# An encoder layer's gate projection cut into four blocks of 960 columns instead of three of 1024 and three chunks

## The chip, the cores and the metric

The kernel runs on one core of a Trainium2 chip. The metric is the device time of one execution in microseconds; the median of three runs of the kernel before is 1906.27 us (1906.04 to 1908.03). The engines are called as in the profile: PE is the matrix engine (PEld its weight loads), DVE the vector engine, ACT the scalar engine, POOL and SP the two others; SP issues nearly all DMAs here.

## What is computed

One encoder layer on 256 tokens of width 4096, all in float32: an input projection, two groups of attention heads, an output projection `w_out`, then a gated per-layer embedding and a last normalisation. The change is in the gated embedding and what follows it:

```python
    x = x + jnp.einsum('bse,ed->bsd', jnp.concatenate([y_a, y_b], axis=-1), w_out[i])

    ple = jnp.einsum('bsc,cd->bsd', p[i], w_ple[i])
    gate = jax.nn.sigmoid(jnp.einsum('bsd,de->bse', rms_norm(x, g_ple[i]), w_ple_gate[i]))
    x = x + ple * gate
return rms_norm(x, g_final)
```

`w_ple_gate` is 4096 x 4096 and `w_ple` 256 x 4096. The gate is (256 x 4096) times (4096 x 4096), the last large product of the kernel.

## The kernel before

**Products in three passes.** Every float32 operand is split into a high half (`hi`, a rounded copy made by ACT) and a low half (`lo`, the difference, made by DVE). A product is the sum of three matmuls: hi x hi, lo x hi, hi x lo (function `mm`). A product here takes 128 rows of contraction (one `kt`, 32 of them), one of the two halves t=0, 1 of the tokens (128 each), and up to 512 columns of weights.

**Steps.** The work is a list of steps. A step loads a piece of weights by DMA into one of four `raw` buffers (`RAW = 4`), converts it to hi and lo into a pair of a ring (three `wp` pairs and, in the gate's blocks, two more slots, `Al2` and `B0`), and multiplies it. A plain step of a block of 1024 columns takes one `kt`: 128 rows by 1024 columns, four products (two token halves, two column halves; PSUM banks M2, X, M3, M4), 12 matmuls.

**Seven products for eight.** In a `Block`, a pair of `kt` can be computed with seven products instead of eight (Winograd's form of Strassen's scheme): four short steps M1, M2 M3, M5 M7, M6 M4, marked `f` in the order. DVE forms four differences of the weights for it, and the sums of the left operand (`x1_sums`, slots `Al0`, `B5`, `Ah1`, `Ah0`) are shared by all blocks. When the last fast product is done, `wide_mid` copies M1 out of its bank and makes four additions; at the end of the block `wide_done` adds the four plain sums, applies tanh (for the sigmoid), multiplies by the embedding and adds to x1, one quarter (128 tokens x 512 columns) at a time, with the sum of squares by ACT in `ss2`. `spread(n, lead, trail, extra)` makes the order of a block: `lead` plain steps, n pairs interleaved with plain steps, `trail` plain steps, and the w_ple step `e` inserted.

**The gate before.** Three blocks of 1024 columns with 7 pairs each, lead 6, trail 4; then a chunk of 512 columns (c=6), a chunk of 256 (c=7) and a chunk of 256 (c=8), all plain (class `Chunk`, whose steps are `Old`). The last chunk runs token half t=0 over all 32 `kt`, keeps the converted weights (`kept`), and then runs t=1, so that t=0's final normalisation (`finish`) and its writes go beside the products of t=1. x1 lies in eight tiles `T0` to `T7` of 512 columns each.

**The end.** `late_gain(c)` multiplies x1's tile c by g_final, loaded by SP (`load_g`) into the slots `Al0` and `B5` once the sums there are dead; behind the last product, `finish(t)` computes the reciprocal root of the mean square by small DVE operations and scales the eight tiles by it (five and the last halves on DVE, two on ACT), each followed by a DMA to the output.

**What sets the order.** Each engine runs its instructions in the order in which they are written out. At build time a small clock in the kernel (`Clock`, with assumed durations) decides when a conversion or a side task is written: `lead` says how many steps ahead conversions may go, `tick` and `advance` let side tasks in, and late gains only when there is slack. So a wait in one engine's list holds up everything behind it there. All operations are recorded by one helper line, L176, and are told apart by tile names without numbers: `hi`, `lo` and `raw` are the ring and load buffers, `m`, `s`, `o`, `t` PSUM banks, `T` the tiles of x1, `B`, `Ah`, `Al`, `Q`, `junk` slots of the SBUF, `st` small statistics.

Of the kernel before, what the change touches and what calls it, by code (L numbers as in the profile page):

```python
# [18 lines left out]
P = 128  # L19
S = 256  # L20
# [177 lines left out]
class Chunk:  # L198
# [4 lines left out]
    def __init__(self, src, nk, n, lhs, banks, done, needs=lambda j: (), per=2, ts=(0, 1), keep=None):  # L203
        self.src, self.nk, self.n, self.lhs, self.banks = src, nk, n, lhs, banks
        self.done, self.needs, self.per, self.ts, self.keep = done, needs, per, ts, keep
        self.ps, self.ring, self.ring_id, self.row = None, WP, None, lambda j: j
# [3 lines left out]
def encoder_layer(ctx: ExitStack, tc: tile.TileContext, x, p, positions, g_mix, w_in, g_q_latent, w_uq,  # L210
# [823 lines left out]
    ss1, ss2 = (stat(NT * n).rearrange("p (t c) -> p t c", t=NT) for n in (8, 9))  # L1034
# [73 lines left out]
    class Step:  # L1108
# [6 lines left out]
        def __init__(self, load, split, run, needs=(), frees=0, time=2.73):  # L1115
            self.load, self.split, self.run, self.needs, self.frees, self.after = load, split, run, needs, frees, None
            self.hold, self.mid = 0, False
            self.time = time
# [4 lines left out]
    class Block:  # L1123
# [9 lines left out]
        def __init__(self, w, lhs, sums, name, order, needs, tags, tmp, ring):  # L1133
# [8 lines left out]
        def step(self, which, *args):  # L1142
            new = Step(*args)
            new.holds = self.holds if which == "M1" else ()
# [11 lines left out]
        def load(self, kt):  # L1156
            kt = self.row(kt)
            r = clock.made(wp.tile([P, 2, Q], F32, tag="raw", name=f"raw_{kt}", bufs=RAW), "raw", RAW)
            for lo, n in ((0, Q), (Q, Q)) if self.late and kt == 16 else ((0, 2 * Q),):
# [24 lines left out]
        def fast_steps(self, j):  # L1184
# [9 lines left out]
            def split1(hi, lo):  # L1194
                if isinstance(self.tmp, tuple):
                    T.extend(slot(b, [2, Q]) for b in self.tmp)
                else:
                    both = slot(self.tmp, [4, Q])
# [122 lines left out]
    blocks = [(512 * c, 512) for c in range(7)] + [(3584, 256), (3840, 256)]  # L1321
    FAST, WIDE = 7, 3
# [21 lines left out]
    def load_g(c):  # L1344
        if not gF:
            gF.extend(slot(tag, [2048]) for tag in ("Al0", "B5"))
# [4 lines left out]
    WIDE_PLE = [dict(zip(((0, 0), (0, 1), (1, 0), (1, 1)), (*PAIRS[2 - k], "t0", "t1"))) for k in range(3)]  # L1351

    def wide_ple(k):
# [3 lines left out]
        def step(kt):  # L1357
            box = []

            def load():  # L1360
                box.append(clock.made(wp.tile([P, 2, Q], F32, tag="raw", name=f"raw_e{kt}", bufs=RAW), "raw", RAW))
                nc.sync.dma_start(box[0].rearrange("p a b -> p (a b)"),
                                  w_ple[kt * P:(kt + 1) * P, 1024 * k:1024 * (k + 1)])

            def run(hi, lo):
                for (t, h), tag in WIDE_PLE[k].items():
                    if kt == 0:
                        ps[t, h] = bank(tag, [Q])
# [5 lines left out]
            return Step(load, lambda hi, lo: split(hi, lo, box[0]), run, ["pT", ("mid", k)], 1)  # L1374

        def out():
            for h in range(2):
                nc.scalar.activation(P4[0, h], ps[0, h], AF.Copy)
# [4 lines left out]

    def wide_mid(k, blk):

        def task():
            e = blk.e = slot("B1", [4, Q])
# [8 lines left out]
    def wide_done(k, blk):  # L1396
        def task():
            e, ps = blk.e, blk.ps
            quarters = ((0, 0, 0, "M2"), (3, 1, 1, "X"), (1, 0, 1, "M3"), (2, 1, 0, "M4"))
            for i, t, h, m in quarters:  # L1400
                nc.vector.tensor_tensor(e[:, i], e[:, i], ps[m], op=ALU.add)
# [594 lines left out]
```

## Time and profile before

| | us |
|---|---|
| median of three runs | 1906.27 |
| profiled execution | 1906.09 |
| its span on the core | 1904.3 |
| PE busy | 1886.7 |
| DVE busy | 1667.5 |
| ACT busy | 1125.3 |
| last product to the end of the span | 12.3 |

The span is from the first to the last instruction; the execution takes 1.8 us more around it. The granted TensorE clock is 0.998 of full speed. A row of the timeline has the start in us, the length, the engine, line, operation, output <- inputs, the shape and a count of merged instructions; a bracket tells how long the engine was idle before it and what released it. Rows of PE show a modelled length that overlaps the next matmul, so the distance between starts is what a matmul costs. A row of a group has the count, the busy time in us, the mean in ns, and the idle time before.

### The profile page before, as it was taken

What the parts mean: (1) busy time and instruction counts of PE and PEld (TensorE: products, weight loads), DVE (VectorE), ACT (ScalarE), POOL (GpSimd) and SP (SyncE); (2) the same over time, 40 slices, a digit from 0 to 9 for tenths busy, and PEclk for the clock granted to TensorE, in tenths of its full rate; (3) what the DMA queues carried; (4) which work ended last, traced back from release to release, by engine and by line L of the source; (5) the groups of instructions that cost most, each with busy time, mean ns of one, the idle gap of its engine ahead of it and who ended that gap; (6) DMA issues with size and microseconds to landing.
All of it is one profiled execution on the core that took longest, in us unless ns stands there. A gap on an engine that the chain in (4) does not pass through costs nothing.

```text
span 1904.3 us, 25920 instructions
## 1 busy us (share of the span) xinstructions
PE 1886.7 (99%) x9430; PEld 1598.9 (84%) x9430; DVE 1667.5 (88%) x2320; ACT 1125.3 (59%) x1523; POOL 29.5 (2%) x41
## 2 busy tenths in 40 slices
PE   9999999999999999999999999999999999999997
PEld 7888888888898888888888999888888888888887
DVE  6999999898878899999998777799988989989865
ACT  7655556564567766556555555656655556665643
POOL 0000000000000000000000011000000000000000
PEclk9999999999999999999999999999999999999999
DMA  8666666666645466676667543566666666666575
GB/s 278 188 207 212 214 215 200 194 217 189 190 139 147 146 196 196 196 216 188 210 199 210 135 131 119 175 216 214 218 203 214 186 201 221 195 216 192 190 234 177
DMA packets 156904, 370.61 MB, mean 195 GB/s; under 512 B 28860, under 2 KB 62760, under 8 KB 156776
## 3 DMA queue, kind: packets, MB, share of 16 engines
q1 hardware_dynamic: 156216, 367.11, 61.9%
q0 software_dynamic: 512, 1.84, 0.3%
q8 instruction: 74, 1.21, 0.3%
q14 instruction: 54, 0.44, 0.1%
q10 hardware_dynamic: 48, 0.02, 0.0%
HBM read 364.72 MB, written 4.19 MB: 194 GB/s over the span
## 4 chain that ended last, share of the span: by engine, by line
PE 89%; DVE 7%; issue 1%; ACT 1%; DMA 1%; DVEq 0%; ACTq 0%
PE m L176 53%; PE t L176 16%; PE s L176 11%; PE o L176 9%; DVE B L176 2%; DVE T L176 2%; DVE lo L176 2%; DMA raw<-in_w_in_dram 1%; ACT hi L176 0%; DVE st L176 0%; ACT T L176 0%; ACT B L176 0%; DVE Al L176 0%; DVE Ah L176 0%; ACT Ah L176 0%
## 5 line engine op out<-in xcount | busy, mean ns | idle before, releaser
L176 ACT ACTIVATE hi<-raw 128x1024 fp32r<-128x1024 f32 (+2 forms) x429 | 412.8, 971 | 303.2 <-PE m L176 96.7
L176 DVE TENSOR_TENSOR lo<-raw,hi 128x1024 fp32r<-128x1024 f32 (+2 forms) x429 | 473.3, 1113 | 87.9 <-ACT hi L176 85.9
L176 PE MATMUL m<-hi,Ah 128*128 128x512 f32 (+2 forms) x764 | 279.9, 379 | 0.1
L176 PE MATMUL m<-hi,Al 128*128 128x512 f32 (+2 forms) x756 | 268.9, 370 | 0.0
L176 PE MATMUL m<-lo,Ah 128*128 128x512 f32 (+2 forms) x643 | 238.6, 371 | 0.7 <-DVE lo L176 0.5
L176 DVE TENSOR_TENSOR B<-raw,B 128x1024 fp32r<-128x1024 f32 (+2 forms) x215 | 199.8, 942 | 17.4 <-ACT B L176 15.8
L176 PE MATMUL m<-hi,B 128*128 128x512 f32 (+1 forms) x678 | 209.2, 364 | 0.0
L176 ACT ACTIVATE B<-raw 128x1024 fp32r<-128x1024 f32 (+1 forms) x131 | 125.2, 965 | 92.9 <-DMA raw<-in_w_in_dram 29.3
L176 PEld LDWEIGHTS m<-hi,Ah 128*128 128x128 f32 x764 | 143.9, 188 | 23.3 <-ACT hi L176 0.6
L176 PEld LDWEIGHTS m<-hi,Al 128*128 128x128 f32 x756 | 141.9, 188 | 23.7
L176 PEld LDWEIGHTS m<-hi,B 128*128 128x128 f32 x678 | 124.3, 189 | 19.7
L176 PEld LDWEIGHTS m<-lo,Ah 128*128 128x128 f32 x643 | 121.2, 189 | 20.4 <-DVE lo L176 2.4
L176 PE MATMUL m<-lo,B 128*128 128x512 f32 (+1 forms) x339 | 123.1, 363 | 0.0
L176 PE MATMUL m<-B,Ah 128*128 128x512 f32 (+1 forms) x427 | 112.7, 363 | 0.4 <-DVE B7b L176 0.4
L176 DVE TENSOR_TENSOR T<-raw,T 128x512 f32<-128x512 f32 (+2 forms) x107 | 85.2, 808 | 5.5 <-ACT T L176 3.9
L176 PE MATMUL m<-B,Al 128*128 128x512 f32 (+1 forms) x323 | 88.8, 351 | 0.0
L176 PEld LDWEIGHTS m<-B,Ah 128*128 128x128 f32 x427 | 73.4, 189 | 13.0 <-DVE B7b L176 0.8
L176 PE MATMUL t<-hi,Ah 128*128 128x512 f32 (+1 forms) x201 | 75.5, 388 | 0.0
L176 ACT ACTIVATE hi<-B 128x1024 fp32r<-128x1024 f32 x53 | 55.5, 1058 | 28.1 <-PE m L176 8.4
L176 PEld LDWEIGHTS m<-lo,B 128*128 128x128 f32 x339 | 64.0, 189 | 9.6 <-DVE lo L176 0.2
L176 DVE TENSOR_TENSOR lo<-B,hi 128x1024 fp32r<-128x1024 f32 x53 | 63.5, 1219 | 2.9 <-ACT hi L176 2.7
L176 PE MATMUL t<-lo,Ah 128*128 128x512 f32 (+1 forms) x167 | 64.6, 387 | 0.0
(502 smaller groups left out, 4135.1 us busy)
## 6 DMA issues: line engine op xcount, KB each, us to landing
raw<-in_w_in_dram SPq DMA_DIRECT2D x359, 512.0 KB, 4.2
raw<-in_w_out_dram SPq DMA_DIRECT2D x128, 512.0 KB, 4.6
raw<-in_w_ple_gate_dram SPq DMA_DIRECT2D x128, 512.0 KB, 4.6
raw_q<-in_w_uq_dram SPq DMA_DIRECT2D x32, 256.0 KB, 3.6
raw_k<-in_w_ukv_dram SPq DMA_DIRECT2D x16, 512.0 KB, 4.1
T<-in_x_dram SPq DMA_DIRECT2D x13, 512.0 KB, 6.2
raw<-in_w_in_dram SPq DMA_DIRECT2D x16, 320.0 KB, 3.0
raw_r<-in_w_uq_dram SPq DMA_DIRECT2D x16, 256.0 KB, 3.6
```

The source lines that it names most:

```text
L176: return do(out, *rest, **named)
```

## The change

The gate becomes four blocks of 960 columns (two halves of 480, `HALF`) with 7, 7, 7 and 6 pairs, and one last chunk of 256 columns. The chunk of 512 and the first chunk of 256 go. Block k covers columns 960k to 960k+959; as x1's tiles are 512 wide, a quarter of 480 columns lies in one or two tiles (`x_parts`), and the sums of squares get 15 partial columns and the last chunk's. The fourth block has lead 5, trail 8, its w_ple step four steps before its end, its quarters in slot `Ah1` (from k=3), and gives up `Al2` and `B0` after its last fast step. The w_ple product of the last chunk goes between the seventh and eighth step of t=0, its halves in the slot of the first sums. The weights kept for t=1 go to other slots, the last of them into `raw` buffers. The g_final loads move into the fourth block, behind the fast step that frees each slot; `late_gain` is made for t=1 alone, five of eight inside the fourth block and three behind it, and `finish(0)` multiplies by r and g in one operation for each tile, all on DVE. In the trailing eight steps and behind them conversions may go nine steps ahead.

```diff
@@ class Block
-        def __init__(self, w, lhs, sums, name, order, needs, tags, tmp, ring):
+        def __init__(self, w, lhs, sums, name, order, needs, tags, tmp, ring, q=512):
+            self.q = q
...
-                self.ps[m] = bank(self.tags[m], [Q])
+                self.ps[m] = bank(self.tags[m], [self.q])
...
-            r = clock.made(wp.tile([P, 2, Q], F32, tag="raw", name=f"raw_{kt}", bufs=RAW), "raw", RAW)
+            r = clock.made(wp.tile([P, 2, self.q], F32, tag="raw", name=f"raw_{kt}", bufs=RAW), "raw", RAW)
...
@@ the gate's sizes
-    blocks = [(512 * c, 512) for c in range(7)] + [(3584, 256), (3840, 256)]
-    FAST, WIDE = 7, 3
+    FAST, WIDE, HALF = 7, 4, 480
+    E_AT = -4
+    FAST_P, LEAD_P, TRAIL_P = (7, 7, 7, 6), (6, 6, 6, 5), (4, 4, 4, 8)
+    END = 2 * WIDE * HALF
...
+    def x_parts(lo, n, t):
+        at, end, got = lo, lo + n, []
+        while at < end:
+            c = at // 512
+            to = min(end, 512 * (c + 1))
+            got.append((at // HALF + c, at - lo, x1[c][:, t, at - 512 * c:to - 512 * c]))
+            at = to
+        return got
...
-            e = blk.e = slot("B1", [4, Q])
+            e = blk.e = slot("Ah1" if k == WIDE - 1 else "B1", [4, HALF])
...
-                    nc.vector.tensor_tensor(xc, u, xc, op=ALU.add)
+                    for _, o, xc in x_parts((2 * k + h) * HALF, HALF, t):
+                        nc.vector.tensor_tensor(xc, u[:, o:o + xc.shape[1]], xc, op=ALU.add)
...
@@ the end
     def late_gain(c):
-        for t in range(NT):
-            nc.vector.tensor_tensor(x1[c][:, t], x1[c][:, t], g_cols(512 * c, 512), op=ALU.mult)
-            yield
-            yield
+        n = 512 if c < 7 else S
+        nc.vector.tensor_tensor(x1[c][:, 1, :n], x1[c][:, 1, :n], g_cols(512 * c, n), op=ALU.mult)
+        yield
...
         for c in range(8):
             xc = x1[c][:, t]
-            if c == 7:
+            if t == 0:
+                nc.vector.scalar_tensor_tensor(xc, xc, r, g_cols(512 * c, 512), op0=ALU.mult, op1=ALU.mult)
+            elif c == 7:
...
@@ the order
     for k in range(WIDE):
-        order = spread(FAST, 6, 4, (-1,))
-        blk = Block(w_ple_gate[:, 1024 * k:1024 * (k + 1)], lhs_x1, x1_s, "x1_sums", order,
-                    lambda kt: [("x1T", kt // 4)], LAST[k], "Ah2", WP + ["Al2", "B0"])
+        order = spread(FAST_P[k], LEAD_P[k], TRAIL_P[k], (-1 if k < WIDE - 1 else E_AT,))
+        blk = Block(w_ple_gate[:, 2 * HALF * k:2 * HALF * (k + 1)], lhs_x1, x1_s, "x1_sums", order,
+                    lambda kt: [("x1T", kt // 4)], LAST[k], "Ah2", WP + ["Al2", "B0"], HALF)
+        top = len(steps) + max(i for i, o in enumerate(order) if o == "f") if k == WIDE - 1 else 10 ** 6
         for tag in ("Al2", "B0"):
-            allow(blk, tag, lambda i: ran[0] >= out_end - 1)
+            allow(blk, tag, lambda i, top=top: ran[0] >= out_end - 1 and i < top)
...
+    for c in range(8):
+        at = fast[8 * (c // 4) + 11] + 1 + (2, 1)[c // 4] * (c % 4)
+        hook(at, lambda c=c: load_g(c))
+        hook(wide_end + 9 if c > 4 else at + 5, lambda c=c: spawn(late_gain(c), True))
+
+    def last(t):
+        return Chunk(cols(w_ple_gate, END, S), 32, S, lhs_x1, ("m2", "m3"), done_g(t), lambda j: (), per=4, ts=(t,),
+                     keep=(stay, t == 0))
+
+    ends = last(0)
+    add(ends, 0, 7)
...
+    add(small)
+    add(ends, 7)
+    add(last(1))
...
-        lead = i + AHEAD + (3 if len(step.ring) > 3 else max(0, min(3, i - (len(steps) - 25))))
+        lead = i + AHEAD + (7 if i > wide_end - TRAIL_P[-1] else 3 if len(step.ring) > 3 else 0)
```

More of the change, by code (lines that the diff above doesn't have):

```diff
@@ L1481, in done_g @@
+            nc.vector.scalar_tensor_tensor(u, u, 1.0, ple[t], op0=ALU.add, op1=ALU.mult)
+            nc.vector.tensor_tensor(xc, u, xc, op=ALU.add)
+            nc.vector.scalar_tensor_tensor(u, xc, 1.0, xc, op0=ALU.mult, op1=ALU.mult, accum_out=ss2[:, t, 15:16])
+            while "part2" not in flags:
+                yield
+            yield from finish(t)
         return task
     def late_gain(c):
[L1484 to L1487 removed]
+        n = 512 if c < 7 else S
@@ new lines, in last @@
+    def last(t):
[3 more added lines that the diff above has]
+    add(ends, 0, 7)
+    small = Chunk(cols(w_ple, END, S), 2, S, lambda kt: (pT[0][:, 0, kt], pT[0][:, 1, kt]), ("m0", "m1"), done_p,
+                  lambda j: ["pT", ("added", WIDE - 1)])
+    small.place = lambda: tuple(zs[0][:, i].rearrange("p (k a) c -> p k (a c)", k=2) for i in range(2))
+    add(small)
```

136 lines of the change are left out of this document (48 added, 88 removed).

## The prediction

> **What bounds the kernel now.** I read the busy shares first, then the shares of the chain of waits, then the busy time of each engine in six stretches (gate blocks 1, 2 and 3; the chunk of 512 and a little of the next; the two chunks of 256; the end).
>
> ```profile
> PE 1886.7 (99%) x9430; PEld 1598.9 (84%) x9430; DVE 1667.5 (88%) x2320; ACT 1125.3 (59%) x1523; POOL 29.5 (2%) x41
> ...
> PE 89%; DVE 7%; issue 1%; ACT 1%; DMA 1%; DVEq 0%; ACTq 0%
> ```
> ```profile
> 1533.00:1621.00 88.00, 88.00 (x394) 72.83 (x393) 78.26 (x102) 51.37 (x61) 0.00 (x0) 1.00 0.66 214
> 1621.00:1709.00 88.00, 88.00 (x390) 72.88 (x389) 80.01 (x94) 54.06 (x64) 0.00 (x0) 1.00 0.64 203
> 1709.00:1797.00 88.00, 88.00 (x389) 72.85 (x389) 79.33 (x94) 52.28 (x62) 0.00 (x0) 1.00 0.62 199
> 1797.00:1849.00 52.00, 51.96 (x253) 43.88 (x252) 36.34 (x42) 27.13 (x38) 0.00 (x0) 1.00 0.65 208
> 1849.00:1892.00 43.00, 43.00 (x359) 42.80 (x357) 27.12 (x50) 17.14 (x23) 0.00 (x0) 1.00 0.57 190
> 1892.00:1904.30 12.30, 0.00 (x1) 0.00 (x0) 5.69 (x21) 1.81 (x3) 0.00 (x0) 0.67 0.44 171
> ```
>
> The columns are stretch, length, then busy time of PE, weight loads, DVE, ACT and POOL, granted clock, DMA share and GB/s. From the first gate product to the last, PE is full at clock 1.00, so the stage costs as many products as it issues, plus what DVE makes late, plus 12 us behind the last product. DVE is at 89 to 91% in the blocks and at 63 to 70% in the chunks behind them: the change turns the light part into a fourth block.
>
> **Part 1, the products.** A step of a block is 12 matmuls (4 products of 3 passes); a pair of steps in seven products saves 3. Before: three blocks of 128 - 7 products, 363 x 3 = 1089 matmuls of 512 columns, the chunk of 512 with 192, and 84 of w_ple: 1365. The two chunks of 256 issue 2 x (192 + 12) = 408. After: 4 x 128 - 27 = 485 products, 1455 matmuls of 480 columns, and 96 of w_ple: 1551; one chunk of 256: 204. The eight transposes stay. What a matmul costs is the distance of two starts, since the durations overlap:
>
> ```profile
> 1564.45 0.39 PE L176 MATMUL m<-hi,Al 128*128 128x512 f32 x1
> ...
> 1575.33 0.39 PE L176 MATMUL m<-hi,B 128*128 128x512 f32 x1
> ```
> ```profile
> 1868.97 23.05 PE m L176 x192
> ```
> ```profile
> 543.11 0.31 PE L176 MATMUL m<-hi,Ah 128*128 128x320 f32 x1
> ...
> 543.98 0.31 PE L176 MATMUL m<-hi,Ah 128*128 128x320 f32 x1
> ```
>
> 48 matmuls of 512 lie in the 10.88 us of the first pair: 226.7 ns each. 192 of 256 took 23.05 us: 120.05 ns. The line through both is 0.4166 ns per column and 13.4 ns fixed; six matmuls of 320 took 0.87 us, 145 ns, where the line has 146.7. So 480 columns, of which before has none, are taken at 213.4 ns; the ends are 120 (as 256 columns) and 226.7 (as 512), and the line decides because the 320 row lies on it. Before: 1365 x 0.2267 + 408 x 0.12005 = 358.4 us. After: 1551 x 0.2134 + 204 x 0.12005 = 355.4. **Term: -3.0 us**, all on the path.
>
> The Trainium skill, "TensorE: Matmul & The Clock Gate", section "Back-to-back issue gap", gives about 81 ns for 128 and 131 ns for 512 columns in a stream of weight loads and products. By it 480 columns would cost 127 ns and 256 columns 98, and the sum 218.7 to 216.6 would be -2.1 us. The trace does not agree (226.7 and 120.05 ns).
>
> **Part 2, a stall that goes.** PE stands still once in the chunks that vanish:
>
> ```profile
> 1848.16 0.36 PE m L176 x3
> 1848.67 0.50 PE s L176 x2
> 1849.53 0.36 PE s L176 x3
> ```
>
> From 1848.16 to 1849.53 are nine matmuls, 1.08 us, in 1.37: 0.3 us lost, with DVE's conversion of the small chunk's weights just then. **Term: -0.3**; if the new small chunk has it again, 0.
>
> **Part 3, DVE in the first block.** Here the cover is thin. Its order of instructions is the same before and after up to the end of this fast stretch.
>
> ```profile
> 1533.54 0.39 PE L176 MATMUL s<-hi,B 128*128 128x512 f32 x1
> ...
> 1600.72 0.39 PE L176 MATMUL m<-lo,B 128*128 128x512 f32 x1
> ...
> 1776.16 0.39 PE L176 MATMUL s<-lo,B 128*128 128x512 f32 x1
> ...
> 1891.72 0.28 PE L176 MATMUL m<-hi,B 128*128 128x256 f32 x1
> ```
> ```profile
> 1547.21 1.22 DVE L176 TENSOR_TENSOR B<-raw,B 128x1024 fp32r<-128x1024 f32 x1 [1.71 <-ACT B L176]
> ...
> 1555.93 0.69 DVE L176 TENSOR_TENSOR Ah<-raw 128x512 f32<-128x512 f32 x1
> ...
> 1563.73 0.69 DVE L176 TENSOR_TENSOR Ah<-raw 128x512 f32<-128x512 f32 x1
> ...
> 1599.22 1.22 DVE L176 TENSOR_TENSOR lo<-raw,hi 128x1024 fp32r<-128x1024 f32 x1
> ...
> 1693.46 0.68 DVE L176 TENSOR_TENSOR B<-B,t 128x512 f32<-128x512 f32 x1
> ...
> 1695.49 0.69 DVE L176 TENSOR_TENSOR B<-B,o 128x512 f32<-128x512 f32 x1
> ...
> 1773.23 1.22 DVE L176 TENSOR_TENSOR lo<-raw,hi 128x1024 fp32r<-128x1024 f32 x1
> ```
> ```profile
> 1546.12 1.06 ACT L176 ACTIVATE B<-raw 128x1024 fp32r<-128x1024 f32 x1 [3.72 <-DMA raw<-in_w_ple_gate_dram]
> ...
> 1605.66 0.58 ACT L176 ACTIVATE B<-m 128x512 f32<-128x512 f32 x1
> ```
> ```profile
> L176 DVE TENSOR_TENSOR lo<-raw,hi 128x1024 fp32r<-128x1024 f32 x63 | 76.5, 1222 | 27.6 <-ACT hi L176 27.5
> ...
> L176 DVE TENSOR_TENSOR lo<-raw,hi 128x512 fp32r<-128x512 f32 x15 | 10.3, 685 | 1.2 <-ACT hi L176 1.2
> ```
>
> One pair and one plain step cost DVE 7.80 us (1555.93 to 1563.73) and PE 33 x 0.2267 = 7.48, so DVE lives on a lead. In pair 7 it ends the lo half at 1600.44 (1599.22 + 1.22) and PE multiplies it at 1600.72: 0.28 us to spare. The two widths give (1222 - 685) / 512 = 1.05 ns per column: an operation of 960 in place of 1024 saves 0.067 us, one of 480 saves 0.034. From 1547.21 to that lo half DVE does 27 wide and 32 narrow ones: 2.9 us less. It starts there when a load has landed and ACT has run (the wait of 3.72 us); with the loads, ACT and the steps ahead 6% shorter I put this start 0.6 us earlier, between 0 (the load does not gain) and 0.8 (it gains as PE does). The stage's first two products, six matmuls, run ahead of the row of 1533.54, so it begins at 1532.18; that lo product is its 299th matmul, and PE comes to it 298 x 0.0133 = 4.0 us earlier. So 0.28 + 2.9 + 0.6 - 4.0 = -0.2: PE waits 0.2 us, with the semaphore on top 0.3 to 0.4. **Term: +0.4**, ends 0 and +1.1. At the tightest place of the third block DVE is done at 1774.45 (1773.23 + 1.22) and PE multiplies at 1776.16: 1.7 us. Narrower operations take 0.3 of it, the four more additions a block, where x1's tiles of 512 cut a quarter in two, 0.3 (0.08 of fixed time each), a gain multiplied inside the fourth block 0.7: cost nothing. Were that cover gone, each microsecond of DVE would be one of PE.
>
> **Part 4, what moves, at nothing.** The g_final loads go into the fourth block's fast stretch. The first of each group waits on SP for the product that frees its buffer, and the weight loads behind it wait too; the next weight queued there is used 18 products (54 x 0.2134 = 11.5 us of PE) later, its conversion takes some 2.3 us of that and a load 4.8:
>
> ```profile
> raw<-in_w_ple_gate_dram SPq DMA_DIRECT2D x96, 512.0 KB, 4.8
> ```
>
> Ten late gains become eight for t=1 alone; t=0's go into its finish. In the trailing eight steps conversions have three buffer pairs only: the step after two plain ones gets its pair when the last fast product is done, and behind ACT's copy (0.58, the row of 1605.66, and 0.2 of semaphores), four additions (1693.46 to 1696.18, 2.6 us at 480) and its own 1.1 us it is ready at +4.5, where PE needs it at +5.3. The last chunk's weights come 12 ahead, 8 loads of 512 KB beside about 30 us of products: some 250 GB/s with the rest of the traffic, more than the 190 to 214 of the stretches above, so this is where rival (c) would bite.
>
> **Part 5, the end.** t=0's finish grows; t=1 must find DVE free.
>
> ```profile
> 1880.58 0.48 ACT L176 ACTIVATE Q<-m,st 128x256 f32<-128x256 f32 x1 [4.10 <-PE m L176]
> 1881.09 0.42 DVE L176 SCALAR_TENSOR_TENSOR Q<-Q,t 128x256 f32<-128x256 f32 x1 [2.83 <-ACT Q L176]
> ...
> 1882.36 0.08 DVE L176 DVE_READ_ACCUMULATOR Q<-T 128x1 f32 x1
> 1882.47 0.59 DVE L176 TENSOR_SCALAR st<-st 128x1 f32<-128x1 f32 x4
> ...
> 1884.44 2.33 DVE L176 TENSOR_SCALAR T<-T,st 128x512 f32<-128x512 f32 x6
> ...
> 1886.69 0.48 DVE L176 SCALAR_TENSOR_TENSOR T<-T,st,B 128x256 f32<-128x256 f32 x1
> ...
> 1892.61 0.42 DVE L176 SCALAR_TENSOR_TENSOR junk<-junk,t 128x256 f32<-128x256 f32 x1 [5.43 <-ACT junk L176]
> ```
> ```profile
> 1850.85 1.29 DVE L176 TENSOR_TENSOR T<-T,B 128x512 f32<-128x512 f32 x2
> ```
>
> t=0's tanh is at 1880.58, its three long operations end at 1882.44. Behind these now come three late gains (1.29 for two, 0.4 for the half one, as the 256 columns of 1881.09), four small operations for the partial sum (0.6, as the four of 1882.47), the small operations (1882.47 to 1884.44, 2.0) and eight multiplications by r and g of 512. Such a one is not in the trace: 0.69 as a plain tensor operation plus the 0.06 by which 0.48 exceeds 0.42, or 0.66 overlapped: 5.3 to 6.0 us. Sum 9.6 to 10.3: ready at 1892.0 to 1892.7, and t=1 calls at 1892.61. **Term: 0**, ends 0 and +0.3. t=1's own operations are the same, and its writes find t=0's gone.
>
> **Sum.** -3.0 - 0.3 + 0.4 + 0 = -2.9 us against the profiled execution, 1906.09 (span 1904.3 and 1.8 around it): 1903.2; the median shown lies 0.2 higher, so **1903.3**. That is -0.15%, and about 0.2% (3.8 us) is what a measurement of this kernel can tell from no change: I forecast no change that counts, from a real gain.
>
> **Rivals.** (a) *480 columns cost more than the line* (the other side). Nothing in the trace runs them. Break-even lies at 1.9 ns more each (3.0 us / 1551), and 0.2% slower needs 4.4 ns; if 480 streamed like 512, 1551 x 0.2267 + 24.5 = 376.1, +17.7 us: 1924. Against it: the 320 row. (b) *DVE bounds more than the first block*: were an operation of 960 no shorter than one of 1024, block 1 would wait 0.3 + 2.9 us more and the others up to 1.5 each: 1904 to 1910. Against it: the two widths' row. For it: 89 to 91% busy. (c) *A load is late*, at the g_final waits or the last chunk: one load's 4.8 us, of which the DVE lead hides some 1.5: +3, 1906.5. The Trainium skill, "DMA: Bandwidth & Descriptors", section "How a descriptor splits into AXI transactions", makes a row cost what its 256-byte pieces cost if it starts aligned: 3840 bytes are 15 of them and each block starts on one, so no row pays extra; this lowers the chance of (c), though no run here shows it. (d) *More gain*: the first block does not wait, and the shorter loads give DVE its lead back: -3.3 and, with 0.5 us of scatter, 1902.3. (e) *A column costs less than the line says.* The change streams 803328 - 796704 = 6624 columns less and issues 18 matmuls fewer; at 0.28 ns per column and the 13.4 fixed the gain would be 2.1 us and the time 1904.2. The rows of 256 and 320 allow 0.39 at the least. The figures that Part 1 cites from the skill would come out there too.
>
> **How the numbers follow.** My forecast 0.63 (1902.6 to 1904.5); (e) 0.02; (d) 0.12, nearly all of it beyond 0.2%; (b) 0.09, (c) 0.08, each with a third above 1910.1; (a) 0.06, nearly all above. So faster 0.12, slower 0.12, same 0.76. The range 1902.2 to 1907.5 leaves out some 0.08 below and 0.12 above.
>
> **What would show it.** Starts of 480 columns 213.4 ns apart; from the first gate product to the end of the last 356.8 us, where before takes 359.7 (1532.18 to 1891.72 + 0.12); a wait of PE for DVE's lo of 0.2 to 0.4 us in the first block and none over 0.3 later; the first small DVE operation of t=1 0.6 us behind the last product's end, as now. I am wrong if the pitch is off the line, if PE waits for DMA or DVE in the fourth block, or if t=0's eight multiplications hold t=1's.

## The result: 1911.0 us, 0.2% slower

The kernel before takes 1907.4 us (median of 11 runs, 1906.0 to 1908.0), the changed kernel 1911.0 (11 runs, 1910.1 to 1913.9): a ratio of 1.0024, 95% interval 1.0016 to 1.0032 (the two medians alone give 1.0019). The forecast was 1903.3, with 1902.2 to 1907.5 as its range. The profiled execution took 1910.42 us, with a span of 1908.6 where the one of before has 1904.3. Its busy shares, and the shares of its chain of waits:

```profile
PE 1890.1 (99%) x9412; PEld 1609.2 (84%) x9412; DVE 1689.5 (89%) x2379; ACT 1137.5 (60%) x1572; POOL 29.5 (2%) x41
...
PE 89%; DVE 7%; DMA 2%; ACT 1%; issue 1%; SPq 0%; DVEq 0%; ACTq 0%
```

By the shares hardly anything has changed. Busy time by stretches (columns as before; the four blocks, the last chunk, the end):

```profile
1531.00:1615.00 84.00, 84.00 (x392) 72.37 (x391) 74.00 (x101) 48.48 (x60) 0.00 (x0) 1.00 0.65 203
1615.00:1700.00 85.00, 84.93 (x392) 73.07 (x391) 76.05 (x96) 52.24 (x68) 0.00 (x0) 1.00 0.73 201
1700.00:1785.00 85.00, 85.00 (x393) 73.45 (x392) 76.80 (x98) 52.11 (x71) 0.00 (x0) 1.00 0.73 206
1785.00:1870.50 85.50, 85.18 (x392) 73.29 (x391) 73.89 (x95) 50.26 (x69) 0.00 (x0) 1.00 0.72 214
1870.50:1895.00 24.50, 24.50 (x205) 24.42 (x203) 22.29 (x49) 11.45 (x27) 0.00 (x0) 1.00 0.31 102
1895.00:1908.60 13.60, 0.14 (x2) 0.00 (x0) 7.56 (x24) 1.81 (x3) 0.00 (x0) 0.60 0.67 257
```

PE is full at clock 1.00 in all four blocks, as it was in three. But 85 us hold 393 matmuls of 480 columns, 216 ns each, where 213.4 were counted on. The time line of PE shows the same over the whole stage: the seventh matmul of 480 columns, the last one, and the last product of the stage.

```profile
1533.07 0.38 PE L176 MATMUL s<-hi,B 128*128 128x480 f32 x1
...
1849.78 0.49 PE L176 MATMUL m<-lo,B 128*128 128x480 f32 x1 [0.32 <-DVE lo L176]
...
1870.29 0.39 PE L176 MATMUL o<-hi,B 128*128 128x480 f32 x1
...
1894.87 0.28 PE L176 MATMUL m<-lasth,B 128*128 128x256 f32 x1
```

From 1533.07 to 1870.29 are 1544 steps from start to start: 218.4 ns with all waits and the eight transposes (0.7 us) in them. Without seven distances that are over 40 ns too long, the mean of the 1551 is 217.2 ns. Starts of 512, 320 and 256 columns are as far apart as before (227, 147 and 120 ns). The second row is the only wait that the profile puts to another engine: the `lo` half of a trailing step of the fourth block, 0.32 us of idle and, by the distances of the starts, 0.5 lost. Ahead of this `lo`, DVE had two late gains and then the four additions of `wide_mid`:

```profile
1844.86 1.28 DVE L176 TENSOR_TENSOR T<-T,Al 128x512 f32<-128x512 f32 x2
1846.07 0.65 DVE L176 TENSOR_TENSOR Ah<-Ah,t 128x480 f32<-128x480 f32 x1
...
1848.57 2.22 DVE L176 TENSOR_TENSOR lo<-raw,hi 128x960 fp32r<-128x960 f32 x2
```

The end, on PE (the last product of t=0), ACT and DVE:

```profile
1883.35 0.28 PE L176 MATMUL m<-lasth,B 128*128 128x256 f32 x1
```
```profile
1878.73 1.06 ACT L176 ACTIVATE lasth<-raw 128x1024 fp32r<-128x1024 f32 x1 [2.64 <-DMA raw<-in_w_ple_gate_dram]
1879.69 1.86 ACT L176 ACTIVATE Ah<-Ah,st 128x480 f32<-128x480 f32 x3
...
1885.52 0.45 ACT L176 ACTIVATE Q<-m,st 128x256 f32<-128x256 f32 x1
...
1895.18 0.47 ACT L176 ACTIVATE junk<-m,st 128x256 f32<-128x256 f32 x1 [8.26 <-PE m L176]
```
```profile
1886.27 0.41 DVE L176 SCALAR_TENSOR_TENSOR Q<-Q,m 128x256 f32<-128x256 f32 x1
...
1891.57 2.74 DVE L176 SCALAR_TENSOR_TENSOR T<-T,st,Al 128x512 f32<-128x512 f32 x4
1894.22 2.73 DVE L176 SCALAR_TENSOR_TENSOR T<-T,st,B 128x512 f32<-128x512 f32 x4
1896.88 0.41 DVE L176 SCALAR_TENSOR_TENSOR junk<-junk,m 128x256 f32<-128x256 f32 x1
```

t=1's tanh is done at 1895.65, but DVE starts on t=1 only at 1896.88, right behind t=0's eighth multiplication. From the last product's end (1894.99) to this row are 1.9 us, where before had 0.77 (1891.84 to 1892.61): 1.1 us more on the path. t=0's finish is late: ACT stood 2.64 us for the last chunk's last weights, and the fourth block's tanh (`Ah<-Ah,st`) and what follows from it on ACT and DVE were queued behind. t=0's last product was done at 1883.47, and with the 0.66 us that t=1's tanh ends behind its last product, t=0's could have ended at 1884.1, some 1.8 us earlier than it did (1885.97). That is an estimate from these rows; no run took this wait away.

Against the profile of before: products +2.9 (1551 x 0.2172 + 24.5 = 361.4 in place of 358.4), the trailing wait +0.6 (with the start behind it), a gap between the first two blocks (starts of 1617.90, 1618.35 and 1618.67) +0.3, the end +1.1, the stall of before that is gone -0.3, and the stage began 0.4 earlier (1533.07 - 6 x 0.217 = 1531.77 in place of 1532.18): +4.2, of 4.3 in the spans. The medians are 3.6 apart, as the profiled run of before lies 1.3 below the median of its kernel and that of the changed one 0.6.

### The profile page after: what moved, and what is told of

Same layout as the page of the kernel before. It is cut to its first block, busy times and chain, and to the rows that moved or that the text cites. A ratio compares the mean times of both kernels' runs of the same rounds, so it can differ in the third digit from the quotient of the medians.

```text
span 1908.6 us, 26023 instructions
## 1 busy us (share of the span) xinstructions
PE 1890.1 (99%) x9412; PEld 1609.2 (84%) x9412; DVE 1689.5 (89%) x2379; ACT 1137.5 (60%) x1572; POOL 29.5 (2%) x41
## 4 chain that ended last, share of the span: by engine, by line
PE 89%; DVE 7%; DMA 2%; ACT 1%; issue 1%; SPq 0%; DVEq 0%; ACTq 0%
PE m L176 50%; PE t L176 18%; PE s L176 12%; PE o L176 9%; DVE T L176 2%; DVE lo L176 2%; DVE B L176 2%; DMA raw<-in_w_ple_gate_dram 1%; ACT hi L176 1%; DVE st L176 1%; DVE Ah L176 1%; ACT T L176 0%; DVE Al L176 0%; DMA raw<-in_w_in_dram 0%; DMA raw<-in_w_out_dram 0%
## 5 line engine op out<-in xcount | busy, mean ns | idle before, releaser
L176 ACT ACTIVATE hi<-raw 128x1024 fp32r<-128x1024 f32 (+4 forms) x420 | 398.6, 957 | 283.6 <-PE m L176 66.9
L176 DVE TENSOR_TENSOR lo<-raw,hi 128x1024 fp32r<-128x1024 f32 (+4 forms) x420 | 455.9, 1095 | 76.5 <-ACT hi L176 74.0
L176 PE MATMUL m<-hi,Ah 128*128 128x512 f32 (+3 forms) x752 | 277.5, 381 | 0.0
L176 PE MATMUL m<-hi,Al 128*128 128x512 f32 (+3 forms) x720 | 258.4, 371 | 0.0
L176 PE MATMUL m<-lo,Ah 128*128 128x512 f32 (+3 forms) x637 | 237.0, 372 | 0.7 <-DVE lo L176 0.3
L176 DVE TENSOR_TENSOR B<-raw,B 128x1024 fp32r<-128x1024 f32 (+4 forms) x222 | 206.5, 943 | 19.1 <-ACT B L176 17.4
L176 PE MATMUL m<-hi,B 128*128 128x512 f32 (+2 forms) x634 | 197.5, 365 | 0.1
L176 ACT ACTIVATE B<-raw 128x1024 fp32r<-128x1024 f32 (+3 forms) x138 | 131.2, 960 | 92.9 <-DMA raw<-in_w_in_dram 27.8
L176 PE MATMUL m<-lo,B 128*128 128x512 f32 (+2 forms) x317 | 115.2, 363 | 0.3 <-DVE lo L176 0.3
L176 PE MATMUL m<-B,Ah 128*128 128x512 f32 (+2 forms) x427 | 112.4, 363 | 0.0
```

The costliest lines, as they stand in the source:

```text
L176: return do(out, *rest, **named)
```

## The experiments

Two streams of matmuls alone settle what 480 columns cost; the other kernels are the changed one with parts undone or sizes changed. Runs of before beside them had medians of 1907.2 to 1907.6 us. The 9 to 11 runs of one kernel lie 2.3 to 4.9 us apart, so a difference of two medians is uncertain by 1 to 2 us: steps of 0.3 to 0.5 us below are not told from none by the times alone, and those of 0.8 and 0.9 barely.

**A stream of matmuls by itself.** A kernel of its own, whose core is this:

```diff
+GROUPS = [("full", 512, 512, 0), ("packed", 480, 480, 0), ("apart", 480, 512, 0), ("na", 496, 512, 0), ...]
+            product(ps[i % 4][:, :n], n, h, tile_at + first + h * step, i % 2, i < 4, i >= PRODUCTS - 4)
```

> This kernel leaves the whole layer out: it loads x, converts it, and streams 21 groups of 72 matmuls in three passes over one pair of weight tiles, with nothing on the other engines meanwhile, and writes x back. The groups differ in columns (512, 496, 488, 480, 472, 464, 448, 416, 384, 352, 320, 256), in the distance of the two halves of a step (480 or 512 elements) and in the first element. Theory A (the 217.2 ns that a 480-column product costs in the changed kernel, in place of 213.4, come from where its moving operand lies: the second half of each step starts at 1920 bytes and the tiles are 3840 bytes apart): 480 columns with halves 512 apart take 213.4 ns, with halves 480 apart about 217; 512 columns with halves 480 apart are slower than 226.7 as well. Theory B (480 columns cost 217 ns wherever they lie; the line through 256 and 512 is wrong between its ends): both 480 groups take 217 ns, the offsets change nothing, and the sizes show where the line breaks (on the line: 496 220.0, 464 206.7, 448 200.0, 416 186.7, 384 173.4, 352 160.0, 320 146.7). Theory C (contention with conversions and loads of the real kernel): both 480 groups take 213.4 here, since nothing else runs.

The time line has, for a group, the first matmul of its second product and of its last; between the two rows lie 66 starts. `packed` and `apart` are 480 columns, `nc` 472, `ng` 384:

```profile
92.99 0.38 PE L55 MATMUL packedx<-hi,wt 128*128 128x480 f32 x1
...
107.27 0.38 PE L55 MATMUL packedz<-hi,wt 128*128 128x480 f32 x1
...
109.92 0.38 PE L55 MATMUL apartx<-hi,wt 128*128 128x480 f32 x1
...
124.22 0.38 PE L55 MATMUL apartz<-hi,wt 128*128 128x480 f32 x1
...
161.86 0.37 PE L55 MATMUL ncx<-hi,wt 128*128 128x472 f32 x1
...
175.93 0.38 PE L55 MATMUL ncz<-hi,wt 128*128 128x472 f32 x1
...
225.72 0.33 PE L55 MATMUL ngx<-hi,wt 128*128 128x384 f32 x1
...
237.16 0.33 PE L55 MATMUL ngz<-hi,wt 128*128 128x384 f32 x1
```

480 columns take 14.28 / 66 = 216.4 ns packed and 14.30 / 66 = 216.7 ns apart, with nothing on DVE, ACT or the queues. So contention (theory C) falls, and the place of the halves (theory A) too. 384 columns take 173.3, where the line has 173.4, but 472 take 213.2, what the line gave for 480. The other groups: 512 columns 226.7 and 320 146.7 (on the line), 496 223.3, 488 225.9, 464 210.1, 448 202.7, 416 188.3, 352 161.1 (1 to 9 ns above it). One thing of theory A is left: 512 columns that start 128 bytes into a tile took 232.4 in place of 226.7, and with halves 480 elements apart 230.4.

**The halves laid apart in the kernel itself.**

```diff
-        shape = [st.ch.per, st.ch.n] if isinstance(st, Old) else [2, st.n]
+        shape = [st.ch.per, st.ch.n] if isinstance(st, Old) else [2, Q]
...
+        return both[:, 0, :, :n], both[:, 1, :, :n]
```

> The changed kernel, with the two halves of every converted step of a block laid 512 columns apart in their tiles, as the three blocks of 1024 had them; nothing else moves. Theory A (address): the distance of two starts of 480 columns falls from 217.2 to 213.4 ns, 1551 x 3.8 ns = 5.9 us less, of which 0.2 to 0.6 may come back as a wait of the first block for DVE: 1904.7 to 1905.5 us beside 1911.0 for the changed kernel. Theory B (size) and theory C (contention): the distance stays at 217 ns and the time at 1910 to 1911.5.

1911.0 us (1910.0 to 1912.4), the same as the changed kernel; the mean distance of 480 columns is 216.7 ns in place of 217.2. Theory A falls a second time. Its profile also shows a wait that the profile of the changed kernel does not have, in the first block. Behind it stand DVE, ACT and a load:

```profile
1582.15 0.48 PE L176 MATMUL m<-lo,B 128*128 128x480 f32 x1 [0.71 <-DVE lo L176]
```
```profile
1580.94 1.16 DVE L176 TENSOR_TENSOR lo<-raw,hi 128x960 fp32r<-128x960 f32 x1 [0.77 <-ACT hi L176]
```
```profile
1579.90 1.90 ACT L176 ACTIVATE hi<-raw 128x960 fp32r<-128x960 f32 x2 [3.15 <-DMA raw<-in_w_ple_gate_dram]
```

This load took 5.9 us from its issue (1573.89) to its landing; the same load of the changed kernel's profile took 4.7.

**Other sizes, other weights, another place in the bank.**

```diff
+GROUPS = [("full", 512, 0, 0), ("sa", 504, 0, 0), ..., ("wa", 480, 32, 0), ("ba", 480, 0, 16), ("one", 480, -1, 0)]
```

> Leaves the whole layer out, as the first stream of matmuls did: 24 groups of 72, halves 512 columns apart. Columns 512, 504, 492, 484, 480, 476, 468, 456, 440, 432, 424, 400, 392, 368, 336, 288, 192, 128; then 480 with the weights at another place in their tile (32, 64, 128 columns further), with the result 16 and 32 columns into its bank, and with one and the same weights for all three passes. Theory B1 (32 cycles of 0.4167 ns on top of the columns for a multiple of 64 up to 384 and for 512, some 40 for what lies between): 288 lies 3 ns or less above the line (133.3), 192 on it (93.4), 504, 492, 484, 476 and 468 lie 2 to 8 ns above (215.0 to 230.0), and neither weights nor bank change the 216 of 480. Theory B2 (the loading of weights collides with the streamed columns): with the same weights for every pass, or with the weights elsewhere, 480 takes 213.4.

The same rows for `sa` (504 columns) and `one` (480, one set of weights for all passes):

```profile
94.71 0.39 PE L58 MATMUL sax<-hi,wt 128*128 128x504 f32 x1
...
109.67 0.39 PE L58 MATMUL saz<-hi,wt 128*128 128x504 f32 x1
...
428.10 0.38 PE L58 MATMUL onex<-hi,wt 128*128 128x480 f32 x1
...
442.39 0.38 PE L58 MATMUL onez<-hi,wt 128*128 128x480 f32 x1
```

504 columns take 14.96 / 66 = 226.7 ns, exactly what 512 take; 480 with one set of weights 216.5, and with weights or result elsewhere 216.6 to 217.8. So the 213.4 of theory B2 did not come: it matters little which weights are loaded, and where they lie. But the group `one` loads weights ahead of every matmul as the plain group of 480 does (time, then busy time and count of PE and of the weight loads):

```profile
147.00:161.00 14.00, 14.00 (x66) 12.12 (x65) 0.00 (x0) 0.00 (x0) 1.00 0.00 1
428.00:442.00 14.00, 14.00 (x67) 12.10 (x66) 0.00 (x0) 0.00 (x0) 1.00 0.00 0
```

Whether the loading itself collides with the streamed columns therefore stays open. B1 holds for 480 and its neighbours but not everywhere: 440 columns took 200.0 ns (the line has 196.7); 400, 424, 368 and 336 took 180.2, 190.0, 166.6 and 153.4 (on the line though no multiples of 64); 288 took 131.7 (1.7 below it), and 192 took 111.7 (18 above it), as 128 did. Why some sizes pay more stays open; that 480 does, in a stream with nothing beside it, is shown.

**t=0's gains and finish as before.**

```diff
-        nc.vector.tensor_tensor(x1[c][:, 1, :n], x1[c][:, 1, :n], g_cols(512 * c, n), op=ALU.mult)
-        yield
+        for t in range(NT):
+            nc.vector.tensor_tensor(x1[c][:, t, :n], x1[c][:, t, :n], g_cols(512 * c, n), op=ALU.mult)
+            yield
...
-            if t == 0:
-                nc.vector.scalar_tensor_tensor(xc, xc, r, g_cols(512 * c, 512), op0=ALU.mult, op1=ALU.mult)
-            elif c == 7:
+            if c == 7:
```

> The changed kernel, but with t=0's gains of g_final multiplied ahead as t=1's are (eight operations more for DVE in and behind the fourth block), and t=0's finish as it was before (six multiplications by r on DVE and two on ACT in place of eight by r and g). Theory: the eight multiplications of t=0, 5.39 us, ended at 1896.88 and held the first operation of t=1, whose tanh was there at 1895.65; with some 1.6 us of late gains and 2.3 us of finish in their place DVE is free at about 1895.5, and the first operation of t=1 follows the tanh at once: from the last product's end to the end of the span 12.4 to 12.6 us in place of 13.6, 1.1 us less in all, if the five more gains inside the block cost PE nothing. Rival: the end is set by t=1's own operations and output writes, or the gains in the fourth block delay its conversions by as much: the time stays within 0.3 us of the changed kernel's.

1911.5 us (1909.9 to 1912.3): nothing gained. In the profile the end is shorter, 12.8 us behind the last product in place of 13.6, but the last product starts at 1897.41 in place of 1894.87, after a stage that began 1 us later and had two waits of the first block, whose instructions are the same as in the changed kernel:

```profile
1560.64 0.49 PE L176 MATMUL m<-lo,Ah 128*128 128x480 f32 x1 [0.64 <-DVE lo L176]
...
1583.04 0.49 PE L176 MATMUL m<-lo,B 128*128 128x480 f32 x1 [0.58 <-DVE lo L176]
```

t=1's first operation followed t=0's last again, now 0.4 us behind the tanh: three of t=0's gains came right ahead of t=0's finish on DVE (1.6 us from 1892.17), and the finish began that much later.

**Widths that lie on the line.**

```diff
-    FAST, WIDE, HALF = 7, 4, 480
+    FAST, WIDE = 7, 4
+    HALF, AT = (512, 512, 512, 384), (0, 1024, 2048, 3072)
```

> The changed kernel with four blocks of 1024, 1024, 1024 and 768 columns in place of four of 960: the same 27 pairs, the same number of matmuls (1161 of 512 columns and 390 of 384 in place of 1551 of 480), the same last chunk and end. Theory B (a size costs what it costs, wherever it lies; the stream alone gave 226.7 ns for 512, 173.3 for 384, 216.3 to 216.7 for 480): 1161 x 0.2267 + 390 x 0.1733 = 330.8 us in place of 1551 x 0.2172 = 336.9, 6.1 us less, so 1904.9 beside 1911.0 for the changed kernel; with PE faster than DVE again, 0.3 to 1.5 us of it may come back as waits for DVE in the first three blocks: 1904.9 to 1906.4. Rival: DVE and the loads set the pace of the four blocks, and the 480 columns only fill time that PE would wait anyway: 1909 us or more, with PE's gaps grown by what the products lost.

1908.5 us (1906.5 to 1911.5): 2.45 below the changed kernel, not 6.1. The sizes cost what the streams said (226.9 and 173.6 ns). The rest of the gain came back as waits of PE, in the profile's sum from 1531 to 1896 (engine, what it waited for: us in total, times, longest):

```profile
PE m L176 <- DVE lo L176: 3.0, 4, 1.3
PE m L176 <- DVE B L176: 0.8, 2, 0.4
PE m L176 <- DVE Al L176: 0.5, 1, 0.5
```

4.3 us of waits, where the changed kernel has 0.3; by the distances of the starts 7.0 us lost in place of 1.0. (The profiled run took 1910.5, 2.0 over the median, so a middling run waits less.) So theory B is right on the price, and the rival is right that DVE and the loads set the pace soon below it.

**The end, on top of these widths.**

```diff
+    EARLY = (0, 2, 4)
...
+        for t in (1, 0)[:1 + (c in EARLY)]:
...
+            if t == 0 and c in EARLY:
+                nc.scalar.activation(xc, xc, AF.Copy, scale=r)
```

> As the kernel with 1024, 1024, 1024 and 768 columns, and besides t=0's gains of the columns 0-511, 1024-1535 and 2048-2559 are multiplied ahead (in the fourth block), so that ACT can do those three of t=0's last multiplications, and DVE five in place of eight. Theory (t=0's finish on DVE holds t=1's first operation by about 1.1 us): that operation follows its tanh at once, and from the last product's end to the span's end it is 12.4 to 12.6 us in place of 13.6: 0.9 to 1.1 us below the kernel with the widths alone. Rival: three more gains in the fourth block make PE wait there by as much (they are 2.0 us of DVE), and the two kernels take the same time.

1908.0 us (1907.2 to 1909.5), 0.5 below the widths alone, which the times do not tell from nothing; the profile shows the step. t=1's first operation now follows its tanh:

```profile
1894.05 0.47 ACT L176 ACTIVATE junk<-m,st 128x256 f32<-128x256 f32 x1 [2.45 <-PE m L176]
```
```profile
1894.56 0.42 DVE L176 SCALAR_TENSOR_TENSOR junk<-junk,m 128x256 f32<-128x256 f32 x1 [1.50 <-ACT junk L176]
```

From the last product's end (1893.86) to DVE's first operation are 0.7 us, as before the change: that t=0's finish held it by 1.1 us is shown. The whole end took 12.9 us, not 12.4 to 12.6: counted from that first operation, the last write landed 0.5 later than in before. In the fourth block PE still waits:

```profile
1834.57 1.14 PE L176 MATMUL m<-Al,Al 128*128 128x384 f32 x5 [0.55 <-DVE Al L176]
...
1843.39 0.44 PE L176 MATMUL m<-B,B7a 128*128 128x384 f32 x1 [0.74 <-DVE B L176]
...
1852.30 0.45 PE L176 MATMUL m<-lo,B 128*128 128x384 f32 x1 [1.33 <-DVE lo L176]
```

**A pair less in the first block of the changed kernel** (`FAST_P` 6, 7, 7, 6).

> The changed kernel with six pairs in seven products in the first block in place of seven (26 in all): three products more, 0.65 us of PE, and some 0.3 us of DVE's lag less per pair left out. Theory: the first block's wait for DVE, which was 0.1 us in the changed kernel's profile and 1.3 and 1.9 us in the profiles of the two variants run so far (whose instructions are the same there), is what scatters the changed kernel's runs from 1910.1 to 1913.9; without it the runs lie within 2 us of each other and the median is 1910.0 to 1911.0. Rival: the scatter comes from elsewhere (the loads at the end, the stages ahead): the runs scatter by 3 us or more, and the median rises by the 0.65 to 1911.6.

1910.45 us (1909.1 to 1912.2). The first block of the profile has no wait left, and the median is 0.5 lower though 0.65 us of products were added; by itself that difference is within the scatter. The runs still lie 3.1 us apart, so the first block's wait is not all of their scatter: in this profile the stage begins at 1533.46, 1.7 us later than in the changed kernel's. The theory's median came, its spread did not.

**g_final's loads on POOL's queue**, on top of the end experiment.

```diff
-        nc.sync.dma_start(g_cols(512 * c, 512), ...)
+        nc.gpsimd.dma_start(g_cols(512 * c, 512), ...)
```

> As the kernel of the end experiment (1024, 1024, 1024 and 768 columns, three of t=0's gains ahead), with the eight loads of g_final issued by POOL in place of SP. In that kernel's profile PE waits 0.74 us at 1834.6 and 0.91 at 1843.4 for weights of the fourth block, and the chain of waits goes through weight loads there. Theory (the g_final loads wait on SP for their buffer, and the weight loads queued behind them come late): both waits go, 1.6 us of PE, and of these 1.0 to 1.6 us reach the end: 1906.4 to 1907.0 beside 1908.0. Rival (the loads are late because their raw buffers come free late, when DVE is done with them, and not because of the queue): the waits stay and the time is the same within 0.4 us.

1910.6 us (1910.1 to 1913.9): 2.5 slower. Neither theory saw this. The profiled run took 1913.2, so the profile shows more than the median lost. Freed from SP's order, four loads of g_final start together, and the weight load beside them takes 7.4 us in the chain of waits, where such loads took 5.0 and 5.8 in the end experiment:

```profile
1827.93 7.40 DMA raw<-in_w_ple_gate_dram
```
```profile
1836.33 0.69 PE L176 MATMUL m<-Al,Al 128*128 128x384 f32 x1 [2.53 <-ACT Al L176]
```

And then the clock falls (stretches of PE's time line: busy time, granted clock, DMA share and GB/s):

```profile
1833.00:1836.00 3.00, 0.80 (x5) 0.96 0.99 382
1836.00:1838.00 2.00, 1.36 (x3) 0.50 0.28 112
1838.00:1840.00 2.00, 2.00 (x8) 0.50 0.72 194
1840.00:1842.00 2.00, 2.00 (x8) 0.50 0.82 204
1842.00:1844.00 2.00, 2.00 (x12) 0.86 0.52 196
1844.00:1846.00 2.00, 2.00 (x13) 1.00 0.53 109
```

The fall of the clock is not in every run: the mean clock is 0.998 in the four fastest of the nine (1910.1 to 1910.4), which are slower than the end experiment all the same, and 0.995 to 0.997 in the five others. Whether the bunching made the weight load late, or POOL's queue by itself, no run separates.

**Two buffer pairs more for the first trailing step**, on top of that.

```diff
-        top = len(steps) + max(i for i, o in enumerate(order) if o == "f") if k == WIDE - 1 else 10 ** 6
+        top = len(steps) + max(i for i, o in enumerate(order) if o == "f") + 3 if k == WIDE - 1 else 10 ** 6
```

> As the kernel with g_final on POOL, and besides the fourth block's conversions may use the two buffer pairs Al2 and B0 for the first trailing step too, where they had three pairs from the last fast product on. Theory (the step after two plain trailing ones gets its buffers only when the last fast product is done, and its conversion then waits behind four additions): the wait of PE for lo at 1852.3, 1.50 us in the end experiment's profile and 0.49 in the changed kernel's, goes or falls below 0.3: 1.2 to 1.5 us less than the kernel with g_final on POOL. Rival: DVE's work sets the time there whatever the buffers, and the wait only moves to a later step or to the last chunk: the same time within 0.4 us.

1909.3 us (1908.4 to 1910.8), 1.25 less. The first trailing step's wait for `lo` (at 1852 in the end experiment; 1.34 us at 1856 in the profile of the kernel this one changes) is gone from the profile; the wait for the late weight load is still there (2.10 us). The theory holds: it was the buffers.

**Six pairs in the first block, on top of that.**

> As the kernel with the buffer pairs, with six pairs in the first block in place of seven (three products of 512 columns more, 0.68 us). Theory (the first block's wait for DVE, 0.9 and 1.9 us in the two profiles of these widths, goes with a pair less): 0.2 to 1.2 us less than the kernel with the buffer pairs. Rival: DVE's lag of the first block is caught up before the end anyway, or it is below 0.68 us on average: the same or 0.3 to 0.7 us more.

1909.0 us (1907.2 to 1911.3), 0.3 less, which the scatter hides; the late load, 3.07 us of wait in this profile, drowns it. The first block of the profile has no wait.

**Five pairs in the narrow block**, g_final on SP again (`FAST_P` 7, 7, 7, 5, with the widths, the end and the buffer pairs).

> As the kernel of the end experiment (1024, 1024, 1024 and 768 columns, three of t=0's gains ahead, g_final on SP again), with Al2 and B0 for the first trailing step, and five pairs in the fourth block in place of six. One pair and one plain step of 768 columns took DVE 6.58 us there (1818.57 to 1825.15) and take PE 33 x 0.1733 = 5.72, so that block lags 0.86 us per pair where one of 1024 lags 0.32. Theory (the narrow block is bound by DVE, and that is where the rest of the widths' gain went): three more products of 384 cost 0.52 us, and the waits at 1834.6 (0.74), 1843.4 (0.91) and 1852.3 (1.50) go: 1.5 to 2.6 us less than the 1908.0, 1905.4 to 1906.5, under the kernel before. Rival (the waits are loads that come late, whatever DVE does): the wait at 1852 goes with the buffers, the two others stay in sum, and the time is 1906.8 to 1908.0.

1905.5 us (1904.4 to 1907.6), ratio to before 0.9991 (0.9982 to 1.0), 2.5 below the end experiment for the pair and the buffer pairs together. The waits at 1834, 1843 and 1852 are gone though products were added. The rival had the first two stay, so DVE's lag is the cause, as the theory has it; in the end experiment's profile SP issued the two weight loads of the chain there, at 1827.54 and 1834.54, right as DVE was done with a raw buffer (1827.51 and 1834.52).

**And six in the first.**

> As the kernel with five pairs in the fourth block, with six pairs in the first in place of seven: three products of 512 more, 0.68 us, against the first block's wait for DVE (0.6 to 1.9 us in the profiles of these widths). Theory (this wait is DVE's lag and changes from run to run): 0 to 0.8 us less than with seven, and the runs lie closer together. Rival: the lag is made good elsewhere: 0.3 to 0.7 us more.

1904.75 us (1903.6 to 1906.7), ratio to before 0.9986 (0.9977 to 0.9995), 0.8 less with 0.68 us of products more; the runs lie no closer together (3.1 us, 3.2 with seven). Its profile has no wait of PE for another engine from 1531 to 1896, and starts its last product 2.3 us earlier than the kernel before (1891.72):

```profile
1889.38 0.28 PE L176 MATMUL m<-lasth,B 128*128 128x256 f32 x1
```

This version is faster than both kernels, than the one before by 0.14%.

**The changed kernel with its last block mended only** (480 columns and 27 pairs kept; `EARLY` and the buffer pairs as above).

> The changed kernel with its 480 columns and 27 pairs, and only the two mends of its last block: three of t=0's gains ahead with ACT's help at the finish, and Al2 and B0 for the first trailing step. Theory (of the 3.6 us that the changed kernel lost to the one before, the products of 480 hold 2.9 and the end and the trailing wait hold 1.1 + 0.5): 1909.2 to 1909.8, still 1.7 to 2.4 us slower than before. Rival (the three more gains inside the fourth block make it wait as much as they save): 1910.5 to 1911.2.

1910.1 us (1908.8 to 1911.3): 0.9 below the changed kernel and 2.6 above the one before, between the theory's times and the rival's. The end follows the tanh, 12.4 us from the last product's end, and the trailing wait is gone, but this profile has the first block's wait at 1581.78 (0.71 us for DVE's `lo`). So some 0.9 of the changed kernel's 3.6 us of loss are its last block, and the 2.6 left are near what the products of 480 columns hold (2.9); the medians are not sharper than that.

## Why the prediction was wrong, step by step

- **Part 1 is the step that failed**: "480 columns, of which before has none, are taken at 213.4 ns ... the line decides because the 320 row lies on it". They cost 217.2 ns in the kernel and 216.4 to 216.7 in a stream alone. The term was -3.0 and came out at +2.9 us. The line does run through 256, 320, 384 and 512 columns, but not through 480; one point on it between the ends was no proof for another. Rival (a) named this, with its break-even at 1.9 ns (3.8 came), and got 0.06. "480 streamed like 512" did not happen either; 504 columns do that.
- The Trainium skill, "TensorE: Matmul & The Clock Gate", section "Back-to-back issue gap", spaces a stream of weight loads and products 131 ns apart for 512 columns. Neither kernel nor stream agrees (226.7), and its table has no size between 256 and 512.
- **Part 2** was right: the stall is gone (-0.3).
- **Part 3** had the right block and the right engine last, but not the place, the size or the whole cause. It put the wait at pair 7, the 299th matmul of the block, from a lag that grows with each pair. By the distances of the starts PE lost 0.1 us in this block in the changed kernel's profile, and 1.3, 1.9 and 1.6 in three profiles with the same order of instructions there (halves apart, t=0's gains, the mended one): more than the term's +0.4 and its end of +1.1. The larger waits lie at the 122nd and the 221st matmul, and none at the 299th. In these three profiles DVE itself stood 0.77, 0.63 and 0.92 us for ACT ahead of the `lo` of the 221st, and ACT for a load that took 5.9, 5.8 and 6.0 us from issue to landing, where it took 4.7 in the profile without the wait. What comes last there is a load, which is rival (c); with DVE's thin lead, most of its delay reaches PE. Why the load takes longer in some runs stays open.
- **Part 4** failed in two places. What it called "ready at +4.5, where PE needs it at +5.3" was the trailing wait, 0.5 us; the buffer pairs removed it. The sum behind +4.5 lacks the two late gains that DVE ran ahead of the four additions (1.2 us from 1844.86 to 1846.07), more than the 0.8 to spare (no run moved them alone). And the last chunk's loads, put "at nothing", were not: the last weights kept ACT 2.64 us, and with it t=0's finish. That load took 5.0 us in the chain of waits, no longer than others; it was issued late (1873.63).
- **Part 5** failed: the term 0, ends 0 and +0.3, was +1.1. The sum of t=0's operations was nearly right (from its first row to t=1's, 1886.27 to 1896.88, 10.6 us, where the forecast has 10.9 to 11.6 from 1881.09 on). What was wrong is the start: the forecast took it from before, where t=0's first operation on DVE lies 11.0 us ahead of t=1's tanh (1881.09 to 1892.10). Here it was 8.9 us ahead (1886.27 to 1895.18).
- **Rival (b)** was priced for operations that are no shorter; the widths experiment shows another form of it: at products on the line DVE gives back 3.6 of 6.1 us. That is shown for blocks of 1024 and 768, not for 960 at 213.4 ns, which no run gave. Had Part 1 been right, the gain would most likely still have been smaller than 2.9.
- **Rival (c)** played a part, as the load in the first block and the one ahead of the last tanh. (d) and (e) did not come.

## What to carry to other kernels

Price a matmul size that the trace lacks by streaming that size alone, not by a line through two others: 472, 476 and 480 columns took 213.2, 213.4 and 216.4 ns, and 504 took as long as 512. Where a second engine is 89% busy, a cheaper product pays only until that engine's lag is reached; here one pair fewer in the narrowest block and two buffer pairs more were together worth 2.5 us, though the former adds products (the pair alone was not run). When a wait ends on an engine, look at what that engine stood for: the first block's wait for DVE ended on a load. When work is moved into a late finish, count from when that finish can start, behind every load and chain that is queued ahead of it.

## What was not expected of the hardware

- The cost of a column is not smooth: on top of 0.4167 ns per column, 512, 424, 400, 384, 368, 336, 320 and 256 columns have 13.3 to 13.5 ns; 472 and 476 have 16.5 and 15.1, 480 16.4 to 17.2, 504 16.7, 488 22.6, 448 16.0, 288 11.7, 192 31.7. For 480 it is nearly the same with other weights, another place of the result, or halves elsewhere (216.4 to 218.2 ns a matmul in all).
- Around a wait of 2.1 to 3.1 us the granted clock of PE fell to half for 3.4 to 6.8 us (0.50 in the rows from 1836 to 1842 above, with a wait of 2.53; the same in the profiles of the two kernels after it, with waits of 2.10, 0.55 more close behind it, and 3.07). Half of the time that PE ran at half rate, 1.7 to 3.1 us, was lost on top, so such a wait cost about twice its length (an estimate). Around waits of 0.3 to 1.34 us the clock did not fall. The Trainium skill, "TensorE: Matmul & The Clock Gate", section "Part 1: The HAM clock gate", has a gate that drops to half rate after an idle window of some 3.4 us; the half rate agrees, and here waits shorter than that window were enough.
- Four loads of 256 KB that spread one row of g_final over all partitions, started together, kept a weight load waiting so long that PE lost 2.5 us; on SP, spaced out between weight loads, no wait at that place is over 0.74 us. The queue differs too, so the bunching alone is not shown to be the cause.
